# Merging six token-major input projections into three of 432 to 512 columns

## The chip, the cores and the metric

The kernel runs on one core of a Trainium2 chip. The metric is the time of one execution on the device in microseconds (us), lower being better. The page and the rows below come from one profiled execution of the kernel before. The engines are TensorE (PE; its weight loads are shown as PEld), VectorE (DVE), ScalarE (ACT), GpSimd (POOL) and SyncE (SP, which issues the DMAs). Lines such as L337 are lines of the kernel before.

## What is computed

The reference is one inference step of two transformer-like layers over 1,152 tokens (1,024 latent and 128 context tokens) of width 1,024. Each layer begins with one input projection whose 2,736 columns feed three mixers side by side:

```python
(cq, ckv, kpe, mq, mk, mv, mo, mi_f, mi_b, mf_f, mf_b,
 gq, gf_f, gf_b, gi, gg) = jnp.split(h @ lp['w_in'] + lp['b_in'], offsets, axis=-1)
...
a_out, mla_st = mla_mixer(cq, ckv, kpe, ...)
m_out, ml_st = mlstm_mixer(mq, mk, mv, mo, mi_f, mi_b, mf_f, mf_b, ...)
g_out, hg_st = hgrn_mixer(gq, gf_f, gf_b, gi, gg, lb, ...)
mix = jnp.concatenate([a_out, m_out, g_out], axis=-1) @ lp['w_out']
```

The first mixer is attention with low-rank queries (cq) and keys and values (ckv). The second, mLSTM, is a matrix memory with queries mq, keys mk, values mv and an output gate sigmoid(mo). The third, HGRN2, is a gated linear recurrence in two directions with values gi and an output gate silu(gg). An output projection, a layer norm and a gated feed-forward block follow. Everything is float32.

## The kernel before

Every product of precision float32 is made of three matmuls: an operand x is kept as hi and lo parts of a reduced type, and `mm3` (L155 to L157) issues hi by hi, lo by hi and hi by lo. The normalised input of a layer lies in `hhi` and `hlo`, eight groups of 128 features by 1,152 tokens. The tokens are nine tiles of 128, or three blocks of 384.

The input projection has two forms. In the feature-major form (`win_fm`, `fm_block`) the weights are stationary and a block of 384 tokens moves, 24 matmuls of 384 columns for a block. In the token-major form (`win_tm`, `tm_group`) the tokens are stationary and the weights move: for each of nine token tiles, 24 matmuls (eight feature groups by three) of as many columns as the group has. There are six such groups: gi, mv, cq, mo and gg have 256 columns and ckv (with kpe and the four gates of the mLSTM) has 176. A group's result goes into one of three PSUM banks (`r_mm`) and is taken out by the group's `evac`.

Weights come in units of at most 1,024 columns. `unit` (L142 to L147) loads one by DMA into a ring of raw tiles (`r_raw`, two here), copies it on ScalarE to the hi tile (L145) and makes the lo tile on GpSimd (L146), in a ring of three hi/lo pairs (`r_w`). A feature-major unit holds one output group for all eight feature groups; a token-major group takes two units.

`phase_a` does this for a layer, in program order: the HGRN2 projections of the first head pair (`g.project(0, ...)`); the group gi; `g.prep(0, ...)`, decays and their scans; `mla_prep`, which holds the groups ckv and cq; `g.states(0, ...)`; then three blocks of `g.outs(0, b, ...)`, the first recurrence, with the projection of the second head pair between them; `ml_gates`; and a written order `0 1 2 p s o0 3 4 o1 5 o2`, in which 0 and 1 are mk, 2 is mv, p, s and o are prep, states and outs of the second head pair, 3 is `ml_states` and 4 and 5 are mq. What the order doesn't name, the gate groups mo and gg (`spill_gate`, 6 and 7), stands at the end, after `mlstm`. In layer 0, `start_mod` adds a matrix-vector product on VectorE in pieces, one `next(bg)` at a time.

A block of outs has seven levels. Each runs four subtractions on GpSimd (L610 to L613), an exponential on ScalarE (L614), three products on VectorE (L615 to L617), matmuls (L623) and two predicated copies on VectorE (L624), with two working tiles `rX`. Besides, prep, states and outs share the ring `rW` of five tiles: prep takes two for each of its six pairs of block and direction, states two and outs three for a block.

A gate group's `evac` adds a bias row (VectorE, L336), applies Sigmoid for mo or Silu for gg (ScalarE, L337), multiplies by a norm row (GpSimd, L338) and stores the result to device memory.

The framework fixes each engine's order of instructions when the program is built: among what its own timeline holds ready it takes the instruction that stands first in the program. So groups late in the program are threaded into earlier stages as far as their data and memory allow. On the chip each engine then keeps that order.

On-chip memory is two stacks, left and right. A `Zone` allocates from one of them in order and is freed at the end of its block; a later tile at the same address waits for the last use of the earlier one. Three overlaps matter here, worked out from the shapes. First, in `phase_b` (attention) the tiles `rf`, `ktmp`, `vtmp` and `qT[0]` lie where `r_w` was, and the tile that receives `w_ukv` (L1012) lies where the bias rows, the norm row and the start of `vaug` (the mLSTM's values) were. Second, the right-hand tiles `kTs[0]` of attention begin just behind `Cst`, the mLSTM's states. Third, the HGRN2 tiles `set0` of the first head pair are on the right and are freed when the first recurrence ends.

Of the kernel before, what the change touches and what calls it, by code (L numbers as in the profile page):

```python
# [20 lines left out]
P = 128  # L21
# [32 lines left out]
TM_NAMES = list(TM_GROUPS)  # L54
TM_COLS = {k: sum(b - a for a, b in v) for k, v in TM_GROUPS.items()}
# [42 lines left out]
class Builder:  # L98
# [11 lines left out]
    def weights(self, z, n=3):  # L110
        self.r_raw = z.ring(n, [P, U])
        self.r_w = Ring([(z([P, U], F32R), z([P, U], F32R)) for _ in range(3)])
# [169 lines left out]
    def start_mod(self, z, j0, j1):  # L282
        raw = z.ring(2, [P, U])
# [45 lines left out]
    def spill_gate(self, l, name, br, nr):  # L329
# [11 lines left out]
        self.win_tm(l, name, evac)  # L341

    def load_mv(self, l, br, vaug):
# [3 lines left out]

        def evac(ps, t):
            V.tensor_tensor(vaug[:, t, :, 0:64], ps.rearrange("p (h c) -> p h c", h=4), b4, op=ALU.add)

        self.row(l, "b_mv", br)
        self.win_tm(l, "mv", evac)
# [14 lines left out]
    def phase_a(self, l):  # L367
# [5 lines left out]
        with ExitStack() as cA:  # L373
            z = Zone(self, cA, f"a{l}")
            self.weights(z, 2)
            self.r_st = z.ring(2, [P, BW])
            brx, nr, mkb = z([P, 304]), z([P, 256]), z([P, 2])
            br = brx[:, 0:256]
# [4 lines left out]
            vaug, mkT = z([P, NT, 4, 65]), z([P, 2, T])  # L383
            with ExitStack() as cH:
                zh = Zone(self, cH, f"hg{l}")
                v = zh([P, NT, 256])
                rW = zh.ring(5, [P, BW])
                g = self.hgrn_setup(l, zh)
                with ExitStack() as c0:
# [4 lines left out]
                    self.row(l, "b_gi", br)  # L394
                    with ExitStack() as c:
                        bg = self.start_mod(Zone(self, c, "gemv"), 16, 24) if l == 0 else iter(())
# [1374 lines left out]
```

## Time and profile before

| | |
|---|---|
| median of 3 runs | 3629.98 us (3626.39 to 3633.87) |
| the profiled execution | 3631.89 us |
| its span | 3630.1 us |
| mean granted clock of PE, share of full speed | 0.952 |
| PE busy, share of the span | 94% |
| DVE / POOL / ACT busy | 62% / 55% / 45% |

A span runs from the first instruction to the last. A busy PE counts each matmul from issue to its modelled end, and matmuls overlap, so the distance between two starts is what one of them costs. `phase_a` of layer 0 runs up to about 595 us and that of layer 1 from about 1,850 to 2,380 us, both overlapped at their ends with attention.

### The profile page before, as it was taken

Reading aid. Unit: us, or ns where it says so; the run is one execution under the profiler, and the core shown is the slowest. Engines: PE = TensorE matmul, PEld = TensorE weight load, DVE = VectorE, ACT = ScalarE, POOL = GpSimd, SP = SyncE. Lnnn points to the kernel's source line nnn. Section 1 sums busy time; section 2 is a strip of 40 time slices with the busy share of each in tenths; the row PEclk is TensorE's granted clock in tenths of the full one; section 3 lists DMA queues with packets and bytes.
Section 4 is the critical chain, followed back from the end, with each engine's and each line's share of the span. In section 5 each row is a group of like instructions: output and inputs, shape, how many; then the busy total and the mean of one; then the engine's idle time right before and its main releaser. Section 6 shows DMA issues by size and latency. Waiting matters only on the chain. (4 is left out here: it accounts for less than half of the span.)

```text
span 3630.1 us, 56094 instructions
## 1 busy us (share of the span) xinstructions
PE 3412.2 (94%) x20556; PEld 3042.1 (84%) x20556; DVE 2253.3 (62%) x4487; ACT 1635.6 (45%) x2877; POOL 2004.7 (55%) x1750
## 2 busy tenths in 40 slices
PE   7999987999989999999899989989989899999989
PEld 7998875776779999988689888877768899999867
DVE  6878878556574444397776678765558544443245
ACT  4264564787343333322272645578863433333111
POOL 3465666777665555401453545557763555556345
PEclk9899976999989999999999999789999899999999
DMA  6212153002452222375422021410043422224232
GB/s 244 73 40 40 41 170 100 18 21 77 126 159 87 85 85 85 97 257 184 159 73 72 30 43 34 131 33 24 21 128 112 126 73 77 75 75 162 71 114 79
DMA packets 331273, 335.77 MB, mean 92 GB/s; under 512 B 191458, under 2 KB 270386, under 8 KB 330996
## 3 DMA queue, kind: packets, MB, share of 16 engines
q1 hardware_dynamic: 330996, 332.19, 29.3%
q8 instruction: 161, 2.64, 0.3%
q14 instruction: 116, 0.95, 0.1%
HBM read 263.54 MB, written 68.56 MB: 91 GB/s over the span
## 5 line engine op out<-in xcount | busy, mean ns | idle before, releaser
L151 POOL TENSOR_TENSOR t<-t,t 128x512 fp32r<-128x512 f32 (+3 forms) x318 | 440.8, 1387 | 374.7 <-ACT t L150 374.4
L150 ACT CAST t<-t 128x512 fp32r<-128x512 f32 (+5 forms) x404 | 270.7, 673 | 692.2 <-PE bank L1449 278.3
L1449 PE MATMUL bank<-hhi,t 128*128 128x256 f32 (+1 forms) x2816 | 570.9, 295 | 7.7 <-DVE t L1349 7.4
L155 PE MATMUL bank<-hhi,t 128*128 128x384 f32 (+1 forms) x1238 | 466.1, 382 | 28.5 <-ACT hhi L145 10.2
L157 PE MATMUL bank<-hhi,t 128*128 128x384 f32 (+1 forms) x1238 | 468.9, 380 | 7.3 <-DVE t L151 7.3
L156 PE MATMUL bank<-hlo,t 128*128 128x384 f32 (+1 forms) x1238 | 470.7, 381 | 5.2 <-POOL hlo L151 4.2
L1449 PEld LDWEIGHTS bank<-hhi,t 128*128 128x128 f32 x2816 | 456.2, 189 | 9.2 <-ACT t L150 7.4
L1187 POOL TENSOR_TENSOR t<-t,t 128x512 fp32r<-128x512 f32 (+1 forms) x304 | 384.5, 1284 | 124.9 <-ACT t L1186 104.0
L1449 PE MATMUL bank<-t,t 128*128 128x320 f32 (+1 forms) x3168 | 435.3, 297 | 4.9 <-ACT t L150 2.2
L1449 PEld LDWEIGHTS bank<-t,t 128*128 128x128 f32 x3168 | 428.9, 191 | 6.3 <-ACT t L150 3.0
L1449 PE MATMUL bank<-hlo,t 128*128 128x320 f32 (+1 forms) x1408 | 415.2, 295 | 0.4 <-DVE hlo L151 0.4
L155 PE MATMUL bank<-t,hhi 128*128 128x256 f32 (+3 forms) x1232 | 387.3, 316 | 13.1 <-DVE t L1107 6.4
L156 PE MATMUL bank<-t,hhi 128*128 128x256 f32 (+3 forms) x1232 | 388.4, 316 | 3.8 <-POOL t L146 3.8
L157 PE MATMUL bank<-t,hlo 128*128 128x256 f32 (+3 forms) x1232 | 388.6, 316 | 0.0
L155 PEld LDWEIGHTS bank<-hhi,t 128*128 128x128 f32 x1238 | 243.4, 197 | 66.8 <-ACT hhi L145 11.1
L1137 DVE TENSOR_REDUCE t<-bank 128x1 f32<-128x384 f32 (+1 forms) x400 | 203.9, 539 | 122.7 <-PE bank L1136 119.5
L156 PEld LDWEIGHTS bank<-hlo,t 128*128 128x128 f32 x1238 | 245.4, 198 | 37.8 <-POOL hlo L151 5.1
L157 PEld LDWEIGHTS bank<-hhi,t 128*128 128x128 f32 x1238 | 244.7, 198 | 38.5 <-DVE t L151 9.7
L155 PEld LDWEIGHTS bank<-t,hhi 128*128 128x128 f32 x1232 | 240.1, 195 | 31.3 <-DVE t L1107 6.6
L1449 PEld LDWEIGHTS bank<-hlo,t 128*128 128x128 f32 x1408 | 265.4, 189 | 0.7 <-issue 0.6
L213 DVE SCALAR_TENSOR_TENSOR t<-t,t 128x1024 bf16<-128x1024 f32 x176 | 239.6, 1361 | 40.1 <-DMA t<-in_w_mod_dram 31.2
L156 PEld LDWEIGHTS bank<-t,hhi 128*128 128x128 f32 x1232 | 240.7, 195 | 19.5 <-POOL t L146 4.0
(356 smaller groups left out, 7291.3 us busy)
## 6 DMA issues: line engine op xcount, KB each, us to landing
t<-in_w_mod_dram SPq DMA_DIRECT2D x96, 512.0 KB
t<-in_w_ffn_in_dram SPq DMA_DIRECT2D x88, 512.0 KB
t<-in_w_ffn_out_dram SPq DMA_DIRECT2D x44, 512.0 KB
t<-in_w_in_dram SPq DMA_DIRECT2D x40, 512.0 KB
shid<-t SPq DMA_DIRECT2D x88, 160.0 KB
sx<-t SPq DMA_DIRECT2D x27, 512.0 KB
t<-sx SPq DMA_DIRECT2D x27, 512.0 KB
shid<-t SPq DMA_DIRECT2D x88, 128.0 KB
```

The costliest lines, as they stand in the source:

```text
L150: self.nc.scalar.copy(hi, src)
L151: (eng or self.nc.gpsimd).tensor_tensor(lo, src, hi.bitcast(F32), op=ALU.subtract)
L155: mm(ps, a[0], b[0], start=first, stop=False)
L156: mm(ps, a[0], b[1], start=False, stop=False)
L157: mm(ps, a[1], b[0], start=False, stop=last)
L213: nc.vector.scalar_tensor_tensor(junk, raw, 1.0, cB[s], op0=ALU.mult, op1=ALU.mult, accum_out=self.modfm[:, l, j, s:s + 1])
L1137: V.tensor_reduce(nm[:, i, b:b + 1] if i < 8 else nm[:, i, 3:4], ps, axis=AX.X, op=ALU.max, negate=True)
L1187: G.tensor_tensor(pl, e, ph.bitcast(F32), op=ALU.subtract)
L1449: mm(ps, a[x][:, k * P:(k + 1) * P], view(y, k, n0, n1), start=first and k == 0 and i == 0, stop=k == 3 and i == 2, skip_group_check=True)
```

## The change

- The six token-major groups become three pairs: gi with ckv (432 columns), cq with mv (512) and mo with gg (512). Each pair has four weight units of two feature groups each; one matmul covers both members, and two evacs share the bank. `r_w` has four hi/lo pairs in place of three.
- gi and ckv come before `prep(0)`, cq and mv after it, so mv leaves the written order, which is now `0 1 p s o0 3 4 o1 5 o2`. The pieces of the matrix-vector product are all drawn in the first pair, with one raw tile in place of two.
- mo and gg are one group at the end. Their bias and norm rows (512 columns each) are new tiles of the zone `ml`, allocated after those of `mlstm`, where `rX` and `rA` or `set1` of the recurrence lie; before, they were tiles of the whole phase.
- `mkT` moves from the left stack, where it lived through the phase, to the right zone `ms`, ahead of `Cst`.
- `rW` has four tiles in place of five. The mask `blk` of `ml_states` (260 columns) is replaced by a view of the HGRN2's mask, so that one product becomes two.

```diff
+TM_PAIRS = (("gi", "ckv"), ("cq", "mv"), ("mo", "gg"))
...
-    def weights(self, z, n=3):
+    def weights(self, z, n, m):
         self.r_raw = z.ring(n, [P, U])
-        self.r_w = Ring([(z([P, U], F32R), z([P, U], F32R)) for _ in range(3)])
+        self.r_w = Ring([(z([P, U], F32R), z([P, U], F32R)) for _ in range(m)])
...
-    def start_mod(self, z, j0, j1):
-        raw = z.ring(2, [P, U])
+    def start_mod(self, z, j0, j1, n=2):
+        raw = z.ring(n, [P, U])
...
-                hi, lo = units[k // 4]
-                w = slice((k % 4) * C, (k % 4 + 1) * C)
+                hi, lo = units[k // 2]
+                w = slice((k % 2) * C, (k % 2 + 1) * C)
...
-    def win_tm(self, l, name, evac):
-        C = TM_COLS[name]
-        u = 10 + 2 * TM_NAMES.index(name)
-        units = [self.unit(self.ins["w_in"][l, u + i][:, :4 * C], 4 * C) for i in range(2)]
+    def win_tm(self, l, i, e0, e1):
+        a, b = [TM_COLS[n] for n in TM_PAIRS[i]]
+        C = a + b
+        units = [self.unit(self.ins["w_in"][l, 10 + 4 * i + u][:, :2 * C], 2 * C) for u in range(4)]
+
+        def evac(ps, t):
+            e0(ps[:, 0:a], t)
+            e1(ps[:, a:C], t)
+
         self.tm_group(units, C, evac)
...
+    def spill_gates(self, l, brx, nr):
+        self.win_tm(l, 2, *[self.gate_evac(l, n, brx[:, 256 * i:256 * (i + 1)], nr[:, 256 * i:256 * (i + 1)])
+                            for i, n in enumerate(TM_PAIRS[2])])
...
-            self.weights(z, 2)
+            self.weights(z, 2, 4)
...
-            brx, nr, mkb = z([P, 304]), z([P, 256]), z([P, 2])
-            br = brx[:, 0:256]
+            mkb = z([P, 2])
...
-            vaug, mkT = z([P, NT, 4, 65]), z([P, 2, T])
+            vaug = z([P, NT, 4, 65])
...
-                rW = zh.ring(5, [P, BW])
+                rW = zh.ring(4, [P, BW])
...
+                        zp = Zone(self, c, f"mp{l}")
+                        br, bv = zp([P, 256]), zp([P, 256])
+                        self.row(l, "b_gi", br)
+                        bg = self.start_mod(Zone(self, c, "gemv"), 16, 24, 1) if l == 0 else iter(())
...
-                        self.win_tm(l, "gi", gi)
+                        ckv, cq = self.mla_prep(l, zp)
+                        self.win_tm(l, 0, gi, ckv)
                         g.prep(0, set0, rW)
-                        self.mark(f"mp{l}")
-                        self.mla_prep(l, Zone(self, c, f"mp{l}"), bg, (brx, nr))
+                        self.win_tm(l, 1, cq, self.mv_evac(l, bv, vaug))
+                        for _ in bg:
+                            pass
...
+                mkT = zs([P, 2, T])
                 Cst = [zs([P, 8, 2, 2, 65]) for _ in range(2)]
...
-                        lambda: self.load_mv(l, br, vaug),
+                        None,
...
-                        lambda: self.spill_gate(l, "mo", br, nr),
-                        lambda: self.spill_gate(l, "gg", br, nr)]
+                        lambda: self.spill_gates(l, zl([P, 512]), zl([P, 512]))]
...
-                order = "0 1 2 p s o0 3 4 o1 5 o2"
+                order = "0 1 p s o0 3 4 o1 5 o2"
...
-                tail = [i for i in "01234567" if i not in order.split()]
+                tail = [i for i in "013456" if i not in order.split()]
...
-        blk = pool([P, 2, 2, 65])
...
+        blk = [self.blk[:, 64 * e:64 * e + 1].unsqueeze(1).to_broadcast([P, 2, 65]) for e in range(2)]
...
-                    V.tensor_tensor(Cst[d][:, n + 1 if d == 0 else n - 1], pv, blk, op=ALU.mult)
+                    for e in range(2):
+                        V.tensor_tensor(Cst[d][:, n + 1 if d == 0 else n - 1, :, e], pv[:, :, e], blk[e], op=ALU.mult)
```

`gate_evac` and `mv_evac` are the evacs of `spill_gate` and `load_mv` without their call of `win_tm`; `mla_prep` returns its two evacs in place of running the groups. The host packs the weights of a pair into four units of 864 or 1,024 columns.

## Rows read from the trace of the kernel before

**Rows 1.** The page, part 1: busy us (share of the span) xinstructions
```profile
PE 3412.2 (94%) x20556; PEld 3042.1 (84%) x20556; DVE 2253.3 (62%) x4487; ACT 1635.6 (45%) x2877; POOL 2004.7 (55%) x1750
```

**Rows 2.** Stretches: us; busy PE, PEld, DVE, ACT, POOL; PE clock; DMA share; GB/s
```profile
82.00:185.00 103.00, 92.70 (x705) 90.67 (x705) 89.63 (x256) 27.80 (x41) 44.83 (x43) 0.88 0.25 78
185.00:310.00 125.00, 123.65 (x852) 113.42 (x850) 94.44 (x219) 77.29 (x102) 79.31 (x105) 1.00 0.13 40
...
338.00:475.00 137.00, 133.19 (x943) 120.12 (x942) 111.01 (x261) 81.32 (x136) 82.98 (x118) 0.96 0.25 59
475.00:590.00 115.00, 90.36 (x469) 80.50 (x467) 100.51 (x289) 52.09 (x121) 88.34 (x91) 0.69 0.56 178
1898.00:1982.00 84.00, 80.45 (x681) 79.68 (x680) 51.46 (x189) 21.12 (x33) 31.78 (x32) 0.98 0.21 63
1982.00:2115.00 133.00, 126.10 (x882) 116.42 (x880) 92.83 (x223) 78.46 (x103) 78.60 (x103) 0.99 0.13 38
...
2141.00:2283.00 142.00, 134.20 (x947) 121.74 (x948) 109.78 (x272) 78.17 (x121) 81.98 (x114) 0.95 0.20 44
2283.00:2380.00 97.00, 86.95 (x462) 78.97 (x460) 76.93 (x269) 56.01 (x136) 52.95 (x62) 0.69 0.47 137
```

**Rows 3.** Timeline of PE, 256 columns, first and last of eight: start us, us
```profile
1920.73 0.28 PE L155 MATMUL bank<-t,hhi 128*128 128x256 f32 x1
...
1921.56 0.28 PE L156 MATMUL bank<-t,hhi 128*128 128x256 f32 x1
```

**Rows 4.** Timeline of PE, 176 columns, first and last of six
```profile
1940.64 0.28 PE L155 MATMUL bank<-t,hhi 128*128 128x176 f32 x1
...
1941.20 0.27 PE L157 MATMUL bank<-t,hlo 128*128 128x176 f32 x1
```

**Rows 5.** Timeline of PE, 512 columns, first and last of six
```profile
1841.31 0.39 PE L156 MATMUL bank<-t,t 128*128 128x512 f32 x1
...
1842.45 0.39 PE L155 MATMUL bank<-t,t 128*128 128x512 f32 x1
```

**Rows 6.** Line 349, the evac of mv: durations ns, first and last start us
```profile
L349 DVE TENSOR_TENSOR t<-bank,t x18: 348/424/427, 300.0 to 2133.6; 128x256 f32<-128x256 f32 x18
```

**Rows 7.** Line 146, lo tile of a unit: durations ns, first and last start
```profile
L146 POOL TENSOR_TENSOR t<-t,t x56: 1702/2390/4357, 15.9 to 3332.5; 128x1024 fp32r<-128x1024 f32 x52, 128x704 fp32r<-128x704 f32 x4
```

**Rows 8.** Timeline of PE, gi of layer 0: [idle before <-releaser]
```profile
88.24 0.58 PE L156 MATMUL bank<-t,hhi 128*128 128x256 f32 x1 [3.75 <-POOL t L146]
```

**Rows 9.** Groups of PE by form, 1982:2115: busy us, mean ns | idle before
```profile
L157 PE MATMUL bank<-hhi,t 128*128 128x384 f32 x120 | 42.4, 353 | 0.0
...
L157 PE MATMUL bank<-t,hlo 128*128 128x256 f32 x39 | 10.9, 280 | 0.0
```

**Rows 10.** Line 535, one of the scans of prep
```profile
L535 DVE TENSOR_TENSOR_SCAN t<-t,t x12: 935/958/3141, 95.5 to 2156.1; 128x384 f32<-128x384 f32 x12
```

**Rows 11.** Timeline of ACT, second recurrence of layer 0
```profile
399.62 1.28 ACT L337 ACT_TABLE_LOAD   x1
400.93 0.42 ACT L337 ACTIVATE t<-t 128x256 f32<-128x256 f32 x1
```

**Rows 12.** Groups of ACT, 2141:2283
```profile
L337 ACT ACT_TABLE_LOAD x13 | 16.7, 1283 | 0.2
```

**Rows 13.** Waits, 2141:2283: us in total, times, longest us
```profile
POOL t L338 <- ACT t L337: 27.8, 10, 6.8
```

**Rows 14.** Groups of PE by form, 2141:2283
```profile
L157 PE MATMUL bank<-t,hlo 128*128 128x256 f32 x121 | 35.7, 296 | 0.0
```

**Rows 15.** Line 338, the norm row of a gate
```profile
L338 POOL TENSOR_TENSOR t<-t,t x36: 723/736/1603, 386.4 to 2305.2; 128x256 f32<-128x256 f32 x36
```

**Rows 16.** Line 1023, first loads of attention into `rf`
```profile
L1023 SPq DMA_DIRECT2D t<-sck x8: 319/455/599, 500.3 to 2300.6; - x8
```

**Rows 17.** Line 1012, load of `w_ukv`, one in each layer
```profile
L1012 SPq DMA_DIRECT2D t<-in_w_ukv_dram x2: 333/354/376, 557.5 to 2356.3; - x2
```

**Rows 18.** Line 1136, first matmuls of attention's peaks
```profile
L1136 PE MATMUL bank<-t,t x304: 220/341/689, 590.4 to 2675.2; 96*128 96x384 f32 x145, 96*128 96x128 f32 x7
```

More of the change, by code (lines that the diff above doesn't have):

```diff
@@ L321, in win_fm, with gate_evac @@
             self.fm_block(w, b, evac)
-    def win_tm(self, l, name, evac):
-        C = TM_COLS[name]
-        u = 10 + 2 * TM_NAMES.index(name)
-        units = [self.unit(self.ins["w_in"][l, u + i][:, :4 * C], 4 * C) for i in range(2)]
+    def win_tm(self, l, i, e0, e1):
[5 more added lines that the diff above has]
+            e1(ps[:, a:C], t)
         self.tm_group(units, C, evac)
-    def spill_gate(self, l, name, br, nr):
+    def gate_evac(self, l, name, br, nr):
         nc = self.nc
@@ L339, in evac, with mv_evac @@
             nc.sync.dma_start(self.s_tm[name][t * P:(t + 1) * P, :], st)
-        self.win_tm(l, name, evac)
-    def load_mv(self, l, br, vaug):
+        return evac
+    def spill_gates(self, l, brx, nr):
+        self.win_tm(l, 2, *[self.gate_evac(l, n, brx[:, 256 * i:256 * (i + 1)], nr[:, 256 * i:256 * (i + 1)])
+                            for i, n in enumerate(TM_PAIRS[2])])
+    def mv_evac(self, l, br, vaug):
         V = self.nc.vector
@@ L346, in load_mv @@
         b4 = br.rearrange("p (h c) -> p h c", h=4)
-        def evac(ps, t):
-            V.tensor_tensor(vaug[:, t, :, 0:64], ps.rearrange("p (h c) -> p h c", h=4), b4, op=ALU.add)
         self.row(l, "b_mv", br)
-        self.win_tm(l, "mv", evac)
+        return lambda ps, t: V.tensor_tensor(vaug[:, t, :, 0:64], ps.rearrange("p (h c) -> p h c", h=4), b4, op=ALU.add)
     def load_mk(self, l, p, bias, mkT):
@@ L393, in phase_a @@
                     g.project(0, set0, early if l == 0 else None)
-                    self.row(l, "b_gi", br)
                     with ExitStack() as c:
-                        bg = self.start_mod(Zone(self, c, "gemv"), 16, 24) if l == 0 else iter(())
+                        zp = Zone(self, c, f"mp{l}")
+                        br, bv = zp([P, 256]), zp([P, 256])
+                        self.row(l, "b_gi", br)
+                        bg = self.start_mod(Zone(self, c, "gemv"), 16, 24, 1) if l == 0 else iter(())
                         def gi(ps, tt):
@@ L462, in hgrn_setup @@
         nc.vector.memset(blk[64:128, 64:128], 1.0)
+        self.blk = blk
         Sall = t([P, 2, 8, P])
@@ L767, in ml_states @@
         at, emt, ws, uw, sc = gates
-        blk = pool([P, 2, 2, 65])
-        V.memset(blk, 0.0)
-        V.memset(blk[0:64, :, 0, :], 1.0)
-        V.memset(blk[64:128, :, 1, :], 1.0)
+        blk = [self.blk[:, 64 * e:64 * e + 1].unsqueeze(1).to_broadcast([P, 2, 65]) for e in range(2)]
         for d, c in ((0, 0), (1, 7)):
@@ L881, in mlstm, with mla_prep @@
             pass
-    def mla_prep(self, l, pool, bg, rows):
+    def mla_prep(self, l, pool):
         nc, ins = self.nc, self.ins
@@ L898, in mla_prep @@
         kvn = self.col(l, "kv_norm")
-        kvrow = rows[0][:, 176:304]
+        kvrow = t([P, P])
         self.row(l, "kv_norm", kvrow)
@@ L909, in rms @@
             V.tensor_scalar(x, x, sm[:, 2:3], None, op0=ALU.mult)
-        bk, bq = rows[0][:, 0:176], rows[1]
+        bk, bq = t([P, 176]), t([P, 256])
         self.row(l, "b_ckv", bk)
@@ L941, in ckv @@
             nc.sync.dma_start(self.s_kp[:, c], tk)
-            next(bg, None)
         self.row(l, "b_cq", bq)
@@ L957, in cq @@
             nc.sync.dma_start(self.s_cq[:, :, c], tmp)
-            next(bg, None)
-        self.win_tm(l, "ckv", ckv)
-        self.win_tm(l, "cq", cq)
-        for _ in bg:
-            pass
+        return ckv, cq
     def phase_b(self, l):
@@ L1709, in pack @@
         units[:, u] = w[..., c0:c0 + P].transpose(0, 2, 1, 3).reshape(DEPTH, P, 1024)
-    for gi, nm in enumerate(TM_NAMES):
-        g = np.concatenate([w[..., p:q] for p, q in TM_GROUPS[nm]], -1)
+    for gi, pair in enumerate(TM_PAIRS):
+        g = np.concatenate([w[..., p:q] for nm in pair for p, q in TM_GROUPS[nm]], -1)
         C = g.shape[-1]
-        for hf in range(2):
-            units[:, 10 + 2 * gi + hf, :, :4 * C] = g[:, 4 * hf:4 * hf + 4].transpose(0, 2, 1, 3).reshape(DEPTH, P, 4 * C)
+        for i in range(4):
+            units[:, 10 + 4 * gi + i, :, :2 * C] = g[:, 2 * i:2 * i + 2].transpose(0, 2, 1, 3).reshape(DEPTH, P, 2 * C)
     a["w_in"] = units
```

## The prediction, made before the run

> **What bounds the kernel now.** I read the page first. PE is busy for 94% of the span [rows 1], so a change that takes matmul time away should pay. But a busy share says nothing of what a stage waits for, so I cut `phase_a`, where every edit lies, into stretches [rows 2]: in each layer the front (gi, prep, ckv, cq), the first recurrence, the second recurrence and the tail (`mlstm` and the gate groups' end, overlapped with attention's first loads). Not listed are 310 to 338 us and 2115 to 2141 us, the stretches where prep of the second pair begins. The reader should see three kinds. In the front of layer 1 and in both first recurrences PE is busy for 95 to 99% of the time. In the front of layer 0 PE and DVE share the load (93 and 90 of 103 us). In the tails DVE leads (100.5 of 115 us) and PE's granted clock is 0.69, the mean of stretches at 1.2 and at 2.4 GHz, because PE has too little to do there. So the same matmul is dear in one place and nearly free in another, and the question is where this change puts its matmuls.
>
> **What a matmul costs.** Distances between starts, at full clock: 256 columns (1921.56 - 1920.73) / 7 = 0.119 us [rows 3]; 176 columns 0.56 / 5 = 0.112 us [rows 4]; 512 columns 1.14 / 5 = 0.228 us [rows 5]. The trace has no 432 columns; on the line between 256 and 512 it is 0.194, and I take that (bounds: 0.119 and 0.228). 176 columns cost almost what 256 do, so gi with ckv saves 0.119 + 0.112 - 0.194 = 0.037 us, times 216 matmuls of a group 7.9 us. Two groups of 256 in one of 512 save 0.009 us, times 216 2.0 us, for two such pairs 4.0. That is 11.9 us of PE time for a layer, 23.8 in all, if PE is what binds.
>
> The Trainium skill ("TensorE: Matmul & The Clock Gate", section "Wait — 56ns, not 53.3ns?") has a warm matmul cost its columns at 2.4 GHz plus about 2.5 ns. By that the two layers' 1,296 saved matmuls would give only 3.2 us; 176 columns would cost 76 ns, and the trace shows 112, so it does not agree here.
>
> **Front.** mv moves in: 216 x 0.119 = 25.6 us more PE work, less 7.9 and 2.0 for the two pairs, +15.7. Every tile now needs four units and all four of `r_w` are in use until the last tile, so the second pair's units are made while that tile runs: four lo tiles of 2.39 us on POOL [rows 7] are 9.6 us, against 4.7 us of last tile and 5.5 of first, a gap of 2 to 3 us. A stall of this kind costs 3.75 us at gi in layer 0 now [rows 8]; it may go or stay. I set these off against each other. Layer 1, where PE is busy 80 of 84 us [rows 2]: +16 (10 to 25). Layer 0 has 10 us of idle PE and a clock of 0.88 to put some of it into: +11 (0 to 21). The first recurrence stands behind these groups in the program, so it starts later by that much.
>
> **First recurrence.** In 1982:2115 it carries 3 x 120 matmuls of 384 columns [rows 9]: 216 are the nine projection blocks, 144 the six blocks of mk. `mkT` now waits for `set0`, so beyond the three blocks for which there are banks mk can't be drawn in: 72 x 0.173 (on the same line) = 12.5 us leave. mv leaves too, 118 x 0.119 = 14 us [rows 9]. Of these 26.5 us I count half, 13, in each layer (0 to 26), since DVE is busy for 92.8 of 133 us and the chain of seven levels for a block remains. What leaves goes into the stretch behind, where prep keeps DVE.
>
> **Between the recurrences.** With five `rW`, one of prep's six pairs can run before the last block of outs returns its tiles; with four, none. A pair is a scan of 0.96 us [rows 10] and seven shorter operations, some 5 us. mv's evac, 9 x 0.42 = 3.8 us of DVE [rows 6], leaves and may give back 2. Net +3 (-4 to 7).
>
> **Second recurrence.** Here mo and gg cost more than their matmuls. Each evac switches ScalarE's tables: a load of 1.28 us, the activation, and another load before the level's exponential can go on [rows 11]; 13 of the first kind fall into the stretch [rows 12]. GpSimd, which starts each level, stands still for 27.8 us of 142 waiting for them [rows 13]. The 3 x 121 matmuls of 256 columns are 43 us of PE [rows 14]. In the change these rows of bias and norm lie where `rX`, `rA` or `set1` of the recurrence are, so only three tiles (banks) of the group can run before its end; the loads, the POOL waits and some 27 us of PE go. What is left is bound by DVE: 109.8 us [rows 2], less 13 evacs of 0.42 [rows 6], plus the split mask (14 products halved: nothing to 14 x 0.42 more; I take 3), 107. The busiest DVE share in a stretch is 0.87 [rows 2]; with fewer stalls I take 0.9: 119 us for 142, -23 (0 to -32). Layer 0: 111.0 gives 120.5 for 137, -16 (0 to -25).
>
> **Tail.** The gates' evacs run here: 18 x 0.42 of DVE, 18 x 0.74 of POOL [rows 15] and up to 27 table loads (Sigmoid, Silu, then Exp for each tile) of 1.28 us, 35 us of ScalarE in a stretch that has 52 to 56 now. DVE in layer 0 becomes 108 of 115 us: +5 for the load. And attention's first loads wait for `r_w`: they start at 500.3 us now [rows 16], some 25 us after the recurrence's end; after the change the group needs nine tiles of 5.5 us behind that end, some 50. Against it, the load of `w_ukv` at 557.5 us [rows 17] waits no longer for `vaug` but for `r_w`; the first peaks come 33 us behind it [rows 18]. I add 3: +8 for each layer (-15 to 28).
>
> The Trainium skill ("ScalarE: Activation LUTs", section "Table sets: the hidden batching unit") says to batch activations by table set, which alternating Sigmoid and Silu does not; its 2.66 us for a switch would make the 27 loads 72 us and the tail ScalarE's. The rows show the activation 1.31 us behind the load's start [rows 11], so I keep 1.28, and the rule counts in the first rival's chance.
>
> **Sum.** Layer 0: 11 - 13 + 3 - 16 + 8 = -7. Layer 1: 16 - 13 + 3 - 23 + 8 = -9. Against the profiled execution: 3631.9 - 16 = 3616 us, 14 below the median of the three runs (3630.0). A measurement of this kernel tells about 0.2% (7 us) from no change.
>
> **Rivals.** *The gate group holds attention back (slower).* If `mlstm`, which comes first in the program, keeps DVE and ScalarE, the group ends only with it, `r_w` comes free late, and attention's loads, splits and projections follow one after another: +30 for each tail in place of +8, 3660 us. For it: DVE is 0.87 busy there [rows 2]. Against: PE is not. It decides once a tail costs over 16. Chance 0.15. *The recurrences keep their pace (slower).* Their chain, not the threaded work, may set it: half of the 65 us gained is lost, 3648 us. For it: DVE is at only 0.70 to 0.81 now; against: the POOL waits. 0.13. *It cancels (same).* mq and attention's early work are drawn into the freed slots and a quarter of the gain goes: 3632 us. 0.20. *PE binds everywhere (faster).* Only the 23.8 us count: 3608 us. 0.17. *The pairs save nothing much (same).* If a matmul pays by the column alone, some 20 of the 23.8 us are missing: 3637 us. It is the skill page's rule as a mechanism; 176 columns at 0.112 us speak against it. 0.03.
>
> **Chances.** My forecast has 0.32 (3606 to 3625). Faster 0.32 + 0.17, with some of the rest 0.50; same 0.22; slower 0.28. The range reaches down to recurrences at a DVE share of 0.95 and up past the second rival into the first: 3590 to 3652.
>
> **What would show it.** Right: 432 columns at 0.19 us; the first recurrence of layer 1 starting 10 to 25 us later relative to its front; no L337 loads inside the second recurrence, and that 15 to 30 us shorter; attention's peaks within 10 us of where they stand now relative to the recurrence's end. Wrong: a second recurrence as long as now, GpSimd waiting on other things; or peaks that come 30 us late, with the gate group's last matmul beside `mlstm`'s.

## The result, and the profile after

The changed kernel takes 3683.55 us (median of 4 runs, 3671.64 to 3687.56) against 3631.12 us: a ratio of 1.0140 with a 95% interval of 1.0114 to 1.0167, slower by 1.4%, some 52 us. The prediction said 3616 us, faster, and its range ended at 3652 us.

The page of the changed kernel, part 1, answers to [rows 1]: PE has 26 us less work and is busy for 92% of a longer span.

```profile
PE 3386.4 (92%) x19260; PEld 2967.7 (81%) x19260; DVE 2247.7 (61%) x4509; ACT 1615.0 (44%) x2858; POOL 1986.6 (54%) x1750
```

Stretches of the changed kernel answer to [rows 2], cut at the edges of the stages: front, first recurrence, gap, second recurrence, tail, layer 0 and then layer 1. Columns: us; busy PE, PEld, DVE, ACT, POOL; PE clock; DMA share; GB/s.

```profile
82.00:195.50 113.50, 104.61 (x494) 87.94 (x492) 89.90 (x261) 22.39 (x35) 47.55 (x48) 0.95 0.21 67
195.50:314.60 119.10, 104.11 (x660) 93.39 (x660) 89.06 (x203) 68.91 (x92) 74.32 (x96) 0.90 0.13 44
314.60:344.40 29.80, 11.22 (x46) 9.21 (x45) 21.95 (x50) 7.17 (x22) 7.96 (x8) 0.50 0.13 10
344.40:480.40 136.00, 122.95 (x760) 108.73 (x759) 97.58 (x258) 48.54 (x90) 70.31 (x101) 0.90 0.16 37
480.40:600.00 119.60, 98.54 (x496) 82.72 (x495) 89.39 (x256) 73.67 (x139) 73.61 (x82) 0.82 0.52 166
1922.00:2033.30 111.30, 109.67 (x540) 93.47 (x538) 69.12 (x224) 26.88 (x40) 42.20 (x46) 1.00 0.18 59
2033.30:2148.60 115.30, 97.96 (x637) 88.93 (x636) 87.42 (x198) 69.58 (x92) 71.50 (x94) 0.89 0.11 35
2148.60:2177.80 29.20, 11.37 (x46) 9.36 (x45) 21.95 (x50) 7.18 (x22) 7.95 (x8) 0.50 0.14 10
2177.80:2310.40 132.60, 122.39 (x758) 108.17 (x757) 97.24 (x256) 44.84 (x77) 67.42 (x97) 0.91 0.12 28
2310.40:2412.00 101.60, 90.29 (x459) 76.18 (x458) 66.95 (x262) 70.46 (x132) 43.97 (x61) 0.84 0.42 129
```

The stretches of [rows 2] are cut at other edges, so here are the first recurrence and the gap of each layer in the kernel before, cut at its own edges of the stages:

```profile
194.50:308.40 113.90, 112.55 (x773) 103.11 (x773) 84.32 (x200) 70.03 (x94) 69.96 (x94) 1.00 0.10 33
308.40:338.30 29.90, 26.25 (x199) 25.24 (x197) 23.83 (x54) 7.14 (x12) 11.38 (x6) 0.92 0.07 22
1998.60:2115.70 117.10, 110.20 (x775) 102.14 (x775) 81.39 (x197) 70.51 (x94) 67.97 (x91) 0.99 0.09 29
2115.70:2141.70 26.00, 21.98 (x173) 21.41 (x171) 20.12 (x46) 9.95 (x15) 8.67 (x9) 1.00 0.11 35
```

The reader should see two things. In the first recurrences PE is busy for 104 and 98 us, where it was 113 and 110, and they last 119 and 115 us for 114 and 117: no shorter. And in the gaps PE does 11 us of work in 30, at half clock, where it did 26 and 22.

To find where the time went I take six marks of each layer from the traces: the third level's first matmul (the planner draws the first two levels ahead), the last copy of the 21st level, the first level of the second head pair, its last copy, the first matmul of attention's peaks, and the first instruction that an engine runs for the output projection. Layer 0 is counted from the start of the program, layer 1 from the copy of its masks, which opens the phase. Lengths in us:

```
                  front  1st rec.  gap  2nd rec.  tail  attention   sum
layer 0  before   194.5   113.9   29.9   136.8   115.3    347.3    937.7
         after    195.5   119.1   29.8   136.0   143.1    334.8    958.3
layer 1  before   147.3   117.1   26.0   141.7    94.4    339.8    866.3
         after    157.4   115.3   29.2   132.6   123.4    332.0    889.9
```

Of the 54 us between the two profiled executions 20.6 and 23.6 lie here; the other 10 lie in the feed-forward blocks, which the change does not touch, and differ as much between other runs. In each layer the tail grows by 28 or 29 us, attention gives 13 and 8 of it back, and the gain that was forecast for the recurrences (29 us in layer 0, 36 in layer 1) is not there: +4 and -11.

Pitches, in the timeline of PE (start us, us), answer to [rows 3] to [rows 5]: 432 columns cost (1947.81 - 1946.63) / 6 = 0.197 us and 512 columns, in the pair cq and mv, (1999.67 - 1998.73) / 4 = 0.235.

```profile
1946.63 0.36 PE L158 MATMUL bank<-t,hlo 128*128 128x432 f32 x1
...
1947.81 0.36 PE L158 MATMUL bank<-t,hlo 128*128 128x432 f32 x1
...
1998.73 0.40 PE L157 MATMUL bank<-t,hhi 128*128 128x512 f32 x1
...
1999.67 0.39 PE L158 MATMUL bank<-t,hlo 128*128 128x512 f32 x1
```

Four lines of the changed kernel by themselves (durations in ns, first and last start in us): the evac of mk, the norm row of the gates (answers to [rows 15]), attention's first loads [rows 16] and its peaks [rows 18].

```profile
L361 ACT ACTIVATE t<-bank,t x12: 562/572/581, 346.3 to 2195.0; 128x384 f32<-128x384 f32 x12
...
L344 POOL TENSOR_TENSOR t<-t,t x36: 722/731/1532, 480.8 to 2404.7; 128x256 f32<-128x256 f32 x36
...
L1026 SPq DMA_DIRECT2D t<-sck x8: 319/402/422, 547.2 to 2399.3; - x8
...
L1139 PE MATMUL bank<-t,t x304: 221/340/689, 623.5 to 2724.6; 96*128 96x384 f32 x144, 96*128 96x128 f32 x8
```

The same line of mk in the kernel before:

```profile
L355 ACT ACTIVATE t<-bank,t x12: 562/575/581, 260.4 to 2095.8; 128x384 f32<-128x384 f32 x12
```

mk was evacuated from 260 us on, inside the first recurrence; it now begins at 346 us, inside the second. As forecast, three of its six blocks are computed in the first recurrence, as many as there are banks; there they wait. Those banks serve every group, so until `mkT` is free no later one can start: the second recurrences now carry 216 matmuls of 384 columns, half of mk and all of mq, against 111 and 106 before (counted in the traces). The gates begin at 481 us in place of 386, attention's loads at 547 in place of 500.

The groups of ACT in the second recurrence of layer 1 and in its tail (2178 to 2310 and 2311 to 2400 us) answer to [rows 12]: the gates' table loads have gone into the tail.

```profile
L343 ACT ACT_TABLE_LOAD x1 | 1.3, 1283 | 0.0
...
L343 ACT ACT_TABLE_LOAD x15 | 19.2, 1283 | 0.3
```

### The profile page after: what moved, and what is told of

Same layout as the page of the kernel before. It is cut to its first block, busy times and chain, and to the rows that moved or that the text cites. A ratio compares the mean times of both kernels' runs of the same rounds, so it can differ in the third digit from the quotient of the medians.

```text
span 3684.0 us, 53475 instructions
## 1 busy us (share of the span) xinstructions
PE 3386.4 (92%) x19260; PEld 2967.7 (81%) x19260; DVE 2247.7 (61%) x4509; ACT 1615.0 (44%) x2858; POOL 1986.6 (54%) x1750
## 5 line engine op out<-in xcount | busy, mean ns | idle before, releaser
L152 POOL TENSOR_TENSOR t<-t,t 128x512 fp32r<-128x512 f32 (+4 forms) x318 | 439.5, 1383 | 385.2 <-ACT t L151 384.5
L151 ACT CAST t<-t 128x512 fp32r<-128x512 f32 (+6 forms) x404 | 270.2, 673 | 655.5 <-PE bank L1452 284.1
L156 PE MATMUL bank<-t,hhi 128*128 128x512 f32 (+2 forms) x800 | 309.5, 389 | 11.6 <-DVE t L925 4.1
L157 PE MATMUL bank<-t,hhi 128*128 128x512 f32 (+2 forms) x800 | 307.9, 385 | 0.0
L158 PE MATMUL bank<-t,hlo 128*128 128x512 f32 (+2 forms) x800 | 306.3, 384 | 0.2 <-POOL hlo L152 0.2
L1188 ACT ACTIVATE t<-bank 128x512 f32<-128x512 f32 (+1 forms) x304 | 174.0, 580 | 57.1 <-PE bank L1187 38.9
L633 PE MATMUL bank<-t 64*128 64x128 f32 x1008 | 148.7, 326 | 48.3 <-DVE t L627 37.2
```

The lines of the kernel that those rows point to most:

```text
L151: self.nc.scalar.copy(hi, src)
L152: (eng or self.nc.gpsimd).tensor_tensor(lo, src, hi.bitcast(F32), op=ALU.subtract)
L156: mm(ps, a[0], b[0], start=first, stop=False)
L157: mm(ps, a[0], b[1], start=False, stop=False)
L158: mm(ps, a[1], b[0], start=False, stop=last)
L633: nc.tensor.matmul(ps[:, jj], X[r, 0, jj], X[r, 1, jj], start=True, stop=True)
```

## The experiments

Five theories came up, the last two on the way. *1*: the late gate group holds attention back. *2*: mk, kept out of the first recurrence and of the gap by `mkT`'s new place, lengthens the second recurrence. *3*: four `rW` tiles are too few. *4*: `mkT` ahead of `Cst` pushes `Cst` under `kTs[0]`, so attention's first keys wait for `mlstm`. *5*: a recurrence has a length of its own, so matmuls inside it are free, and the same matmuls in the front are paid in full. Ratios are to the kernel before, run on the same chip.

**The gates' rows from memory that is always there** (changed kernel; the gates get other bias and norm numbers):

```diff
-        self.row(l, "b_" + name, br)
-        self.row(l, "n_" + name, nr)
...
-                        lambda: self.spill_gates(l, zl([P, 512]), zl([P, 512]))]
+                        lambda: self.spill_gates(l, *[self.hhi[:, i, 0:512].bitcast(F32) for i in range(2)])]
```

> The changed kernel, with the four bias and norm rows of the gate group taken from a part of hhi that is always there (the gates get other numbers, the work is the same but for eight row loads). Theory 1 (the gate group, which can finish only behind the recurrence, holds attention's first loads through r_w): the group is drawn into the second recurrence, attention's loads start within 35 us of the recurrence's end and not 67 and 87 us behind it, and of the 54 us lost 25 to 50 come back: 3635 to 3660 us. Theory 2 (mk, pushed out of the first recurrence and out of the gap behind it, keeps the second recurrence long): that stretch is full of matmuls already, the group only makes it longer, and less than 15 us come back: above 3668 us. Theory 3 (four rW tiles): no change, 3675 to 3690 us.

Measured: 3683.81 us, 1.0148 (1.0123 to 1.0173): nothing came back. Attention's loads do start early, at 496.2 us in place of 547.2, but the second recurrences take 149.8 and 148.7 us (136.0 and 132.6 in the changed kernel), the tails 124.0 and 105.0 (143.1 and 123.4). What the tail gives, the recurrence and, in layer 0, attention take. The time lies in the ranges of theories 2 and 3. The timeline of ACT in layer 1 shows theory 4's wait: attention's cast into its keys stands idle for 10.47 us until `mlstm`'s last matmul on `Cst` (L853).

```profile
2404.17 1.33 ACT L151 CAST t<-t 32x384 fp32r<-32x384 f32 x3 [10.47 <-PE bank L853]
```

**The late rows alone, in the kernel before:**

```diff
-                        lambda: self.spill_gate(l, "mo", br, nr),
-                        lambda: self.spill_gate(l, "gg", br, nr)]
+                        lambda: self.spill_gate(l, "mo", zl([P, 256]), zl([P, 256])),
+                        lambda: self.spill_gate(l, "gg", zl([P, 256]), zl([P, 256]))]
```

> The kernel before, with one part of the change: the bias and norm rows of mo and gg are tiles allocated behind mlstm's, over tiles of the recurrence. Theory 1: the second recurrences become shorter by up to 20 us each without the gates, but attention's first loads wait for both groups; the net is a loss of 20 to 30 us in each layer, 3670 to 3690 us. Theory 2: the second recurrence has room then and gets shorter by what the tail loses: 3625 to 3650 us. Theory 3: no loss, 3632 us or less.

Measured: 3647.72 us, 1.0037 (1.0023 to 1.0050). The second recurrences get shorter by 13.3 and 11.7 us, the tails longer by 21.6 and 29.9. The time lies in theory 2's range, though the tails lose more than the recurrences gain, as theory 1 had it. In this kernel late gates cost about a quarter of the loss.

**`mkT` ahead of ml_gates' tiles, and four `rW` in the kernel before:**

```diff
                 gates = [zm([P, NT, 8]) for _ in range(4)] + [zm([P, 2, 2, NT])]
+                mkT = zm([P, 2, T])
...
-                mkT = zs([P, 2, T])
```

```diff
-                rW = zh.ring(5, [P, BW])
+                rW = zh.ring(4, [P, BW])
```

> The changed kernel, with mkT allocated ahead of ml_gates' working tiles, at the same address, so that mk waits for the first recurrence's end alone and not for ml_gates. Theory 2: mk's 25 us of matmuls fill the gap of 31 us behind the first recurrence, in which PE is busy for 12.5 us at half clock, and the second recurrence gets 15 to 25 us shorter in each layer: 3635 to 3655 us. Theory 1: mk moves, the levels keep nearly their pace, and attention still waits for the gate group: at most 15 us come back, 3668 to 3685 us.

> The kernel before with four rW tiles in place of five, and nothing else. Theories 1 and 2: within 8 us of the kernel before, 3625 to 3640 us. Theory 3 (the fifth tile is what lets prep of the second pair run ahead): 15 to 25 us for each layer, 3660 to 3680 us.

Measured: 3662.13 us, 1.0088 (1.0064 to 1.0112), and 3616.27 us, 0.9964 (0.9940 to 0.9987). The first goes in theory 2's direction, with 21 us, short of its range: mk's first evac comes at 313.8 us in place of 346.3, the gaps shrink to 23.7 and 23.2 us and the second recurrences to 126.6 and 128.3. The second came out below every range: in the kernel before, where mv's matmuls fill the gap, a working tile fewer did no harm. That ends theory 3 for this kernel. Five tiles in the changed kernel were not tried. There the gap waits for `rW`: in layer 0 VectorE stands idle in prep (L540) for 3.3 us until a tile of the last outs is stored, and the scan behind it (L547), at 336.4 us, is what GpSimd waits for before the states (L568).

**`kTs[0]` behind `Cst` again** (changed kernel; `qT[1]` goes to the right, in front of it):

```diff
-            ze([P, 576])
+            qT[1] = pair(ze, [97, T])
+            ze([P, 552])
...
-            kTs[1], kC[1], qT[1], vs[1] = pair(z, [97, T]), pair(z, [97, P]), pair(z, [97, T]), z([P, 10, 130], F32R)
+            kTs[1], kC[1], vs[1] = pair(z, [97, T]), pair(z, [97, P]), z([P, 10, 130], F32R)
```

> The changed kernel, with qT[1] of attention moved to the right-hand stack, so that kTs[0] begins behind Cst again, as before the change. Theory 4 (mkT put ahead of Cst pushes Cst under kTs[0], so attention's first keys wait for mlstm's last reading of Cst): in layer 0, where Cst is read until 581.9 us and the gate group ends at 557.8 us, the first peaks come up to 25 us earlier; in layer 1, where the group ends last (2405 against 2389 us), nothing: 3655 to 3675 us. Theory 2 (matmul time lost in the first recurrence and behind it): within 8 us, 3675 to 3690 us.

Measured: 3697.01 us, 1.0172 (1.0153 to 1.0191). That is above every range, and no gain: the peaks of layer 0 come at 622.0 us (623.5), those of layer 1 no earlier. Theory 4's wait is real, but taking it away brings nothing. (The edit has a price of its own: attention of layer 0 lasts 350 us with it, against 335.)

**`mkT` ahead of `set0`,** so that mk can be drawn in as early as before; `rX` and `rA` are allocated after the front to make the room. Then the same **with the two edits above** (gate rows, `kTs[0]`):

```diff
+                cK = ExitStack()
+                mkT = Zone(self, cK, f"mk{l}", "right")([P, 2, T])
                 with ExitStack() as c0:
...
-                mkT = zs([P, 2, T])
...
             cM.close()
+            cK.close()
...
-        rX = z.ring(2, [P, 2, BW])
-        rA = z.ring(2, [P, 2, 3, P])
+        rX, rA = Ring([]), Ring([])
+
+        def late(z2):
+            rX.tiles = z2.ring(2, [P, 2, BW]).tiles
+            rA.tiles = z2.ring(2, [P, 2, 3, P]).tiles
```

> The changed kernel, with mkT allocated on the right ahead of set0, so that mk waits for nothing and can be drawn into the first recurrence as before the change (rX and rA are allocated later, to make the room). Theory 2: PE is filled in the first recurrence, the second one is 20 to 30 us shorter than in the changed kernel, and 25 to 50 us of the 54 come back: 3633 to 3658 us. Theory 1 (gate group) or 4 (Cst under kTs[0]): both holds stay, attention's peaks come when the group and mlstm are done, which is earlier by what the recurrences gain, at most 20 us in all: 3660 to 3680 us.

> The changed kernel, with three things undone together: gate rows taken from a part of hhi that is always there (the gates get other numbers, same work), kTs[0] behind Cst, mkT ahead of set0. What is left of the change: three pairs, mv in the front, four r_w pairs, four rW, the split mask. If theories 1, 2 and 4 together are the whole loss, the 12 us of matmul time a layer show at last: 3595 to 3630 us. If moving mv into the front costs more than the pairs save, 3630 to 3650 us. If the loss has another cause, above 3660 us.

Measured: 3663.24 us, 1.0080 (1.0061 to 1.0099), and 3663.17 us, 1.0085 (1.0067 to 1.0104). The first is in the range of theories 1 and 4, the second in that of another cause: theories 1, 2 and 4 together are less than half of the loss. What was left in the second of these, above all mv in the front, remained to explain the rest. The stretches of the first of the two, both recurrences of each layer:

```profile
209.60:325.10 115.50, 111.10 (x734) 102.17 (x734) 81.77 (x185) 65.26 (x90) 66.24 (x90) 0.99 0.11 35
...
347.20:466.70 119.50, 95.30 (x499) 81.09 (x498) 106.13 (x261) 31.55 (x67) 65.53 (x93) 0.66 0.10 9
...
2033.90:2149.30 115.40, 113.92 (x747) 105.18 (x748) 81.60 (x185) 62.57 (x85) 65.06 (x90) 0.99 0.10 33
...
2169.40:2288.70 119.30, 91.41 (x470) 79.55 (x471) 105.53 (x262) 37.60 (x73) 61.26 (x92) 0.57 0.10 9
```

The first recurrences last 115 us with 111 and 114 us of PE work, 119 and 115 with 104 and 98 in the changed kernel. The second ones last 119 us with hardly a matmul of the projection in them (15 and 7), at a clock of 0.66 and 0.57. So some 110 to 120 us is what a recurrence takes by itself: theory 5; what sets that length was not tried. But the fronts now take 209.6 and 176.0 us (195.5 and 157.4): three and a half blocks of the second head pair's projection are drawn into them besides mv (301 and 317 matmuls of 384 columns against 216 and 230). mk follows in the first recurrence, its first evac at 260.8 us.

**mv back at its old place,** and **mv and mk both back** (`mkT` ahead of `set0` besides). cq and mv are packed as groups of their own; mv's bias row is a part of `hhi`:

```diff
-                        self.win_tm(l, 1, cq, self.mv_evac(l, bv, vaug))
+                        self.win_one(l, 0, cq)
...
-                        None,
+                        lambda: self.win_one(l, 1, self.mv_evac(l, self.hhi[:, 0, 512:768].bitcast(F32), vaug)),
...
-                order = "0 1 p s o0 3 4 o1 5 o2"
+                order = "0 1 2 p s o0 3 4 o1 5 o2"
```

> The changed kernel, with its second pair taken apart: cq stands alone in the front, mv alone at its old place in the written order (its bias row is taken from a part of hhi, other numbers, same work). Theory 5 (a recurrence needs some 115 us for its chain whether PE is full or not, so matmuls inside it cost nothing, and the same matmuls in the front cost their full time): the front of layer 1 gets 10 to 20 us shorter, the first recurrence stays at 115 to 120 us, layer 0, whose front is DVE's too, gains 0 to 10: 3655 to 3675 us. Theory 1 (only the gate group's place in the tail): 3680 us or more.

> The changed kernel with mv at its old place (as in the run before) and mkT ahead of set0, so that both can be drawn into the first recurrence. Left of the change: the pairs gi with ckv and mo with gg, the gates behind the recurrence, Cst under kTs[0], four r_w, four rW. Theory 5: first recurrence 115 to 120 us with both in it, second one near 120 us, and only the tail still loses 20 to 28 us, against a front that is 8 us shorter: 3630 to 3652 us. If mk and mv are not what was lost, as much as with mkT ahead alone: 3655 us or more.

Measured: 3680.71 us, 1.0140 (1.0117 to 1.0163), and 3625.13 us, 0.9980 (0.9967 to 0.9992). The first misses theory 5's range and lies in theory 1's, the second is below theory 5's. mk alone gave back 20 us, mv alone 3, both together 58. Alone, mv shortens the fronts by 21.3 and 20.8 us, and all of it is lost again in the second recurrences, which take 159.3 and 157.1 us. There mk is evacuated from 321.3 us on, and mv only behind it:

```profile
L361 DVE TENSOR_TENSOR t<-bank,hhi x18: 423/425/426, 339.6 to 2191.5; 128x256 f32<-128x256 f32 x18
```

mv has nothing of its own to wait for. It stands behind mk in the program and in the rings `r_w` and `r_mm`, and mk waits for `mkT`; that the rings are what holds it is read from the code and was not tried apart. With both back, the first recurrence carries mk and half of mv in layer 0 and nearly all of mv in layer 1 (four and eight of its nine evacs begin in it) in the same 113 and 116 us (here its two rows, then those of the second recurrence):

```profile
181.30:293.90 112.60, 108.92 (x764) 101.45 (x764) 83.62 (x195) 65.48 (x91) 68.59 (x93) 0.98 0.10 30
...
1995.10:2111.50 116.40, 114.62 (x806) 105.70 (x807) 79.28 (x193) 57.47 (x78) 64.43 (x88) 0.97 0.08 25
...
322.50:446.80 124.30, 111.94 (x658) 97.08 (x659) 106.88 (x266) 42.52 (x90) 69.40 (x100) 0.84 0.21 40
...
2131.10:2256.60 125.50, 107.60 (x617) 91.75 (x618) 108.16 (x271) 40.51 (x80) 69.18 (x96) 0.82 0.15 26
```

**mv in the front, alone, in the kernel before:**

```diff
                         self.mla_prep(l, Zone(self, c, f"mp{l}"), bg, (brx, nr))
+                        self.load_mv(l, br, vaug)
...
-                order = "0 1 2 p s o0 3 4 o1 5 o2"
+                order = "0 1 p s o0 3 4 o1 5 o2"
```

> The kernel before, with mv alone moved: it stands right behind cq in the front and no longer in the written order. Theory 5: its 25.6 us of matmuls are paid in layer 1 (15 to 26 us) and in part in layer 0 (0 to 12), nothing comes back in the first recurrence: 3645 to 3670 us. If the first recurrence is bound by PE, what the front loses comes back there: 3625 to 3640 us.

Measured: 3656.31 us, 1.0075 (1.0050 to 1.0100), 25 us. The fronts take 26.9 and 24.6 us more, mv's 25.6 us; the first recurrences stay at 117.7 and 114.8 us (113.9 and 117.1). About half of it comes back behind them. In the kernel before mv is evacuated from 300.0 us on [rows 6], at the end of the first recurrence, and more than half of its matmuls in layer 0 and nearly half in layer 1 lie in the gap. Without them mq is drawn in earlier, its first evac at 319.7 us in place of 340.2, and the gaps shrink to 8.1 and 8.7 us (29.9 and 26.0); in layer 0 the second recurrence takes 12.5 us more. The rows of the gaps:

```profile
339.10:347.20 8.10, 8.10 (x54) 7.49 (x52) 4.82 (x25) 4.57 (x8) 3.65 (x6) 1.00 0.08 27
...
2157.60:2166.30 8.70, 8.70 (x61) 8.26 (x59) 4.57 (x25) 4.50 (x8) 3.04 (x5) 1.00 0.22 81
```

So mv is paid in full in the front, as theory 5 says, and the time lies in its range; but mv's old place was only about half free. With `mkT` ahead of `set0` mv out of the front is worth 1.0% (1.0080 and 0.9980 above), with intervals too wide to tell that from the 0.75% here.

**Gate rows, and `kTs[0]`, once more,** now in the kernel with mv and mk back:

> As the run with mv and mk back in the first recurrence, and the gate group's rows taken from hhi besides, so that the gates can be drawn into the second recurrence too (other numbers in the gates, same work). The second recurrence took 124 and 126 us there, and attention's peaks came 136 and 124 us behind it, against 137, 142, 115 and 94 us in the kernel before. If the late group costs by holding attention: the recurrence gets up to 18 us longer, the tail 20 to 29 us shorter, 3605 to 3620 us. If it only moves the same work: within 6 us of 3625 us. If mlstm's use of Cst is the hold, no tail shortens.

> As the run with mv and mk back in the first recurrence, and kTs[0] of attention behind Cst besides (qT[1] goes to the right-hand stack). If Cst under kTs[0] holds attention's keys: 5 to 20 us less, 3605 to 3620 us. If the gate group and mlstm's own length set the peaks, as the same edit in the changed kernel showed: within 8 us of 3625 us.

Measured: 3630.41 us, 0.9989 (0.9975 to 1.0003), and 3633.20 us, 0.9997 (0.9982 to 1.0012). Undoing either hold gains nothing that can be measured (0.9980 without these edits). With early gates the second recurrences take 142.9 and 152.7 us (124.3 and 125.5) and the tails 113.7 and 93.8 (135.7 and 123.7): in this kernel the gates' work has one price in either place.

**The pair gi and ckv alone, in the kernel before** (four `r_w`, three `rW`, `rX` and `rA` allocated late; first with one `rku` and `ml_states` copying through `r_st`, then with the split mask in their place):

```diff
-                        self.win_tm(l, "gi", gi)
-                        g.prep(0, set0, rW)
-                        self.mark(f"mp{l}")
-                        self.mla_prep(l, Zone(self, c, f"mp{l}"), bg, (brx, nr))
+                        ckv, cq = self.mla_prep(l, Zone(self, c, f"mp{l}"), nr)
+                        self.win_gc(l, gi, ckv)
+                        g.prep(0, set0, rW)
+                        self.win_tm(l, "cq", cq)
...
-        self.r_w = Ring([(z([P, U], F32R), z([P, U], F32R)) for _ in range(3)])
+        self.r_w = Ring([(z([P, U], F32R), z([P, U], F32R)) for _ in range(4)])
...
-                rW = zh.ring(5, [P, BW])
+                rW = zh.ring(3, [P, BW])
```

> The kernel before with only the pair gi and ckv (432 columns, four units), four r_w pairs, three rW and one rku; mk, mv and the gate groups as before. By the theories the front loses 8 us of matmuls in each layer, nothing else moves, and w_ukv's load waits for r_w in place of vaug, so attention's peaks may come up to 20 us earlier: 3575 to 3620 us. Theory 3 (the number of rW sets the recurrences' pace): the recurrences get longer by over 10 us each, above 3640 us.

> As the earlier kernel with only the pair gi and ckv in the kernel before (four r_w, three rW), but ml_states keeps its own tiles (the split mask makes the room), so that mq and the gates no longer wait for it. Theory 5: the front loses 8 us of matmuls in each layer, the recurrences keep mk, mv and the gates, w_ukv's load waits for r_w in place of vaug: 3590 to 3620 us. If three rW cost what the pair saves: 3625 to 3640 us.

Measured: 3633.99 us, 0.9987 (0.9971 to 1.0002), and 3606.28 us, 0.9939 (0.9918 to 0.9960). In the first, mq's evac comes 98 us late in layer 0 (437.7 us against 340.2), behind `ml_states`, whose use of the ring `r_st` stands ahead of mq's in the program. The second beats both kernels. Taken apart, without the pair, with three and with four `r_w`:

> The kernel before with three rW, rX and rA allocated later, and the split mask; three r_w, six groups. It is the kernel with the pair gi and ckv (3606 us) less the pair and the fourth r_w pair. If the pair's matmul time is what that kernel gained: 3622 to 3638 us. If fewer rW tiles give the gain, as four in place of five did by 14 us: 3600 to 3618 us.

> The run above with four r_w pairs, still six groups. If the pair's matmul time is the gain: as the run above, within 6 us. If the fourth r_w pair is (w_ukv's load then waits for r_w and not for vaug, so attention's peaks come earlier): 3600 to 3615 us.

Measured: 3652.17 us, 1.0050 (1.0029 to 1.0070), and 3645.99 us, 1.0032 (1.0016 to 1.0049). The first lies above both of its ranges, the second some 6 us below the first, about as it should if the pair is the gain. So the pair is the gain, about 0.9%, more than its matmuls explain: in layer 1 the front is 10.4 us shorter with the pair than without, in layer 0 44.3 us, of which 23.2 are lost again in the first recurrence and the gap. The pair also brings ckv ahead of prep; what that is worth, in layer 0's front above all, was not tried apart.

At last four `rW` in the kernel with the pair, beside the kernel with three:

```diff
-                rW = zh.ring(3, [P, BW])
+                rW = zh.ring(4, [P, BW])
...
-        rku = pool.ring(2, [P, 2, 4, 64])
+        rku = pool.ring(1, [P, 2, 4, 64])
```

> The kernel with the pair gi and ckv (3606 us), with four rW in place of three; one rku in place of two, the norm row behind Cst and some small tiles merged make the room. If a fourth rW is worth what three cost without the pair (18 us): 3580 to 3598 us. If the pair's kernel doesn't wait for rW: 3600 to 3612 us.

> The kernel with the pair gi and ckv and three rW once more, beside the one with four on the same chip: 3600 to 3614 us, 0.5 to 0.8% below the kernel before.

Measured: 3605.06 us, 0.9918 (0.9903 to 0.9932), and 3612.39 us, 0.9940 (0.9924 to 0.9957). The pair's kernel doesn't wait for `rW`: the two intervals overlap.

## Why the prediction was wrong, step by step

- **What a matmul costs** was right for 432 columns (0.197 for 0.194, 7.3 us a group for 7.9). Two groups of 256 in one of 512 save next to nothing: 2 x 0.119 - 0.235 = 0.003 us, 0.6 us for the 2.0 of the sum.
- **Front,** +11 and +16, measured +1.0 and +10.1: within its bounds, in part by luck. By itself mv costs its full 25 us there (the run that moves mv alone), but 37 and 40 fewer matmuls of the second head pair's projection were drawn into the fronts (216 and 230 for 253 and 270), some 7 us that no term had.
- **First recurrence,** "Of these 26.5 us I count half, 13, in each layer": this step failed. It measured +5.2 and -1.8. The first recurrences took 108 to 126 us in either layer of all runs, whatever PE had to do in them: it was busy for 93 to 123 us of that. (Two exceptions, both in layer 0: 128.7 us with `mkT` ahead of ml_gates, and 143.6 in the kernel with the pair and four `rW`, whose third level was drawn ahead too.) PE's busy share of 95 to 99% was read, by half, as a bound; it was filling.
- **Between the recurrences,** +3, measured -0.1 and +3.2: right as a length, by luck. "With four, none" was wrong: three of prep's six scans run before the first recurrence ends, with four tiles (286.3, 298.2 and 305.7 us in layer 0) as with five. But with four they are all of one direction, and the levels wait for the first scan of the other, at 336.4 us. What one step earlier says is wrong too, "What leaves goes into the stretch behind, where prep keeps DVE". The half of mk that leaves does not go there. `mkT` lies not only over `set0` but also over ml_gates' working tiles, so mk's first evac comes at 346.3 us, behind the gap, and at 313.8 us where `mkT` is allocated ahead of them; in the gap PE is busy for 11 of 30 us, at half clock.
- **Second recurrence,** -16 and -23, measured -0.8 and -9.1: failed by the same omission. The bound itself held: 120.5 and 119 us were worked out from DVE at a share of 0.9, and the run in which mk was done earlier shows 119.5 and 119.3 at 0.89 and 0.88. In the changed kernel half of mk and all of mq arrive there, 216 matmuls of 384 columns, 37 us at the forecast's 0.173, where there were 111 and 106.
- **Tail,** +8, measured +27.8 and +29.0 up to the peaks, of which attention gives back 12.5 and 7.8. The picture is that of the first rival, its price too; its cause is not. Early gates in the changed kernel gave nothing, and in the kernel with mk and mv back the gates cost the same early and late; only in the kernel before did late gates cost 0.4%. The tail is longer because the gates' work lies there, and with what attention gives back it would be paid for if the second recurrence were the 120 us of the forecast.
- **The second rival,** that the recurrences keep their pace, was right as a mechanism for the first recurrence, at 0.13, and too cheap at 3648 us. It halved the gain of the recurrences but left mk where it costs nothing.
- `Cst` under `kTs[0]`, which the prediction did not see, showed as a wait, and taking it away gained nothing.

So the loss is one of place, and the two halves need each other: mk and about half of mv, some 37 us of matmuls a layer, stood free of charge in the first recurrence, and the rest of mv in the gap. mv was put into the front, where it is paid; mk was locked out by `mkT` and held mq back with it, so that both are paid in the second recurrence. Putting one back alone returns 20 or 3 us, putting both back 58. What stays open: the 10 us of the profiled executions outside these phases; whether a fifth `rW` would shorten the gap of the changed kernel; why four `rW` are better than five in the kernel before (0.9964) and three without the pair, with the split mask and late `rX`, worse (1.0050); and why the kernel with mk and mv back, which keeps a pair worth 0.9%, is only 0.2% faster than the kernel before.

## What to carry to other kernels

A stage that shows PE at 95 to 99% may still be set by another chain, with PE's work threaded into its gaps: compare its length in a kernel with less of that work before counting what leaves as a gain. When a tile moves in memory, list every tile that it now overlaps and who uses those last, and then everything that stands behind its first user in the shared rings, because that waits too. Two edits that block each other show too little when undone one at a time (20 and 3 us here, of 58), so undo them together as well.

## What the hardware showed that was not expected

The second recurrences of 119.5 and 119.3 us ran at a granted clock of 0.66 and 0.57, with PE busy for 95 and 91 us; the kernel before took 137 and 142 us at 0.96 and 0.95 [rows 2]. The shortest of all runs, in layer 1 of the first kernel with only the pair gi and ckv, ran at 0.60:

```profile
2145.00:2255.50 110.50, 82.92 (x431) 70.43 (x431) 94.16 (x221) 37.69 (x68) 65.42 (x95) 0.60 0.09 6
```

A stretch can be at its shortest while its clock is a mean of the two levels, 1.2 and 2.4 GHz, with PE idle for a fifth of the time or more. (That kernel gains nothing by it: what left the recurrence lies in its tail, 147 us in place of 94.) And a matmul of 432 columns costs 0.197 us next to 0.119 for 256 [rows 3] and 0.112 for 176 [rows 4]: below 256 columns width was worth next to nothing here, so joining the group of 176 to one of 256 saves 7.3 us of matmuls and joining two of 256 0.6.
